# A layer step on one core: the running sums of the gates stored in DRAM by head and then by chunk

## The chip, the cores and the metric

The kernel runs on one core of one Trainium2 chip. The metric is the device time of one execution, in microseconds. Runs of one kernel differ by about 0.1% here: the three runs of the kernel before lie between 1456.16 and 1457.99 us.

## The reference, cut to what matters

One layer of a hybrid decoder is computed for a prompt of 1024 tokens and for 8 samples of one token each. All of it is float32. A combined projection `h @ w_in` (1024 to 10256 columns) feeds two branches. Branch B is a gated delta rule with 8 heads of 128 x 128, evaluated in chunks:

```python
proj = h @ w_in
hA, cA, bA, zA, qkv, zB, beta_raw, alpha_raw, gA, gB = jnp.split(proj, offs, axis=-1)
...
g = -jnp.exp(a_log) * jax.nn.softplus(alpha_raw + dt_bias)        # one number per token and head
...
gc = jnp.cumsum(g, axis=-1)                                       # running sum inside a chunk, per head
decay = jnp.exp(jnp.where(causal, gc[..., :, None] - gc[..., None, :], -jnp.inf))
a_mat = jnp.where(strict, jnp.einsum('bhncd,bhnsd->bhncs', kb, k) * decay, 0.0) + jnp.eye(C)
...
attn_qk = jnp.einsum('bhncd,bhnsd->bhncs', q, k) * decay
q_dec = q * jnp.exp(gc)[..., None]
```

So `gc` is needed twice for every head: as a row (the index s runs along a row of `decay`) and as a column. The change concerns the rows.

## The kernel before, in words

**Work and stages.** TensorE computes the projection as jobs of 128 columns. Each job has three groups of 344 tokens, and each float32 product is made of three passes of a rounded part and a remainder (`xh`/`xl` with `whi`/`wlo`), so a job is 3 x 8 x 3 matmuls into PSUM tiles called `pm_t`. For each head h there is a K, a Q and a V job, a job for a gate and one for z. Between about 90 and 815 us of the span these jobs run, and the delta rule of the heads runs between them: its matmuls write PSUM tiles called `pa_t`. From 815 us on come products of the second branch, the output projections and the tail, which do not use the part that is changed.

**Order.** Every engine works through its instructions in the order in which they were written. That order is settled when the program is made: `Sched` keeps a modelled clock of each engine, and generators ("strands", run by `slot()` after every k step of a job) are advanced when their modelled time has come. `Paced.__getattr__` adds to these clocks at every call. A `tensor_copy` on VectorE, for one, adds 100 ns and its elements per partition divided by 1.92; a DMA is modelled by its size alone, as 1100 ns, the bytes divided by 360, and 700 ns.

**The running sums.** `ba_gen` computes the gates once, near 85 us. A matmul with a triangular matrix gives `gc`, a tile of 128 partitions (position in the chunk) by 8 chunks by 8 heads (`gcf` is the same with 64 columns, chunk by chunk). TensorE transposes it to `gcr` (64 rows of 128), and SyncE (SP) writes that to `gsc` in DRAM, 64 rows of 512 bytes in the order chunk, head.

**The broadcasts.** `gc_rows(h)` is an access pattern that reads the 8 rows of head h and repeats them for all 128 partitions: 512 KB land in SBUF. It is loaded twice for every head, both times on SP's DMA queue. `decay_gen` (after the K job of the head) loads it into `DA`; ScalarE (ACT) adds the negated column to it in 8 instructions (`DA<-DA,ngc`), VectorE (DVE) masks it, and ACT takes the exponential, so that `DB` and `DA` become the two decay matrices. `delta_gen` loads it again into `gcB`; `qd_gen` lets ACT take the exponential and DVE multiply q by it. ACT and DVE also empty the PSUM tiles of the jobs, split the weights (`whi`, `wlo`), and do the small steps of the recurrence: `vn` is copied out of PSUM by ACT, and TensorE needs it for the next two matmuls (`pa_t<-vn,kd` and `pa_t<-vn,DA`). A head also has loads and stores that invert a triangular matrix through DRAM (`sA`, `At`, `sT`, `Ts`), and the samples' step has a broadcast of its own: `rsc[h]`, 8 rows of 128 that lie one after another, is written by SP and read back for all partitions into `rB`.

Nearly all instructions are recorded at line 128, the helper `Paced`, so the profile is read by tiles.

Of the kernel before, what the change touches and what calls it, by code (L numbers as in the profile page):

```python
# [8 lines left out]
F32 = mybir.dt.float32  # L9
# [7 lines left out]
P = 128  # L17
# [5 lines left out]
NH = 8  # L23
C = 128
NC = S // C
# [136 lines left out]
def hybrid_step(  # L162
# [9 lines left out]
    V, A, PE, GP, SY = (Paced(e, n, sched) for e, n in (  # L172
        (nc.vector, "V"), (nc.scalar, "A"), (nc.tensor, "PE"), (nc.gpsimd, "GP"), (nc.sync, "SY")))
# [9 lines left out]
    def ps_aux():  # L183
        return psum["pa"].tile([P, 512], F32, tag="pa", name="pa_t")

    def tt(out, a, b, op):
        V.tensor_tensor(out=out, in0=a, in1=b, op=op)

    def ts(out, a, s1, s2=None, op0=ALU.mult, op1=None):
        if s2 is None:  # L190
            V.tensor_scalar(out=out, in0=a, scalar1=s1, scalar2=None, op0=op0)
        else:
            V.tensor_scalar(out=out, in0=a, scalar1=s1, scalar2=s2, op0=op0, op1=op1)

    def stt(out, a, s, b, op0, op1):
        V.scalar_tensor_tensor(out=out, in0=a, scalar=s, in1=b, op0=op0, op1=op1)
# [6 lines left out]
    def act(out, in_, func, **kw):  # L203
        A.activation(out=out, in_=in_, func=func, **kw)
# [57 lines left out]
    gc = cpool.tile([P, NC, NH], F32, name="gc")  # L262
# [10 lines left out]
    gsc = dram.tile([NC * NH, C], F32, name="gsc")  # L273
# [11 lines left out]
    def transpose(out, in_):  # L285
        n = in_.shape[0]
        PE.transpose(out, in_, ident[:n, :n])
# [465 lines left out]
    def ba_gen():  # L753
        ap_ = bp
        ban = ap_.tile([P, 9, 16], F32, name="ban")
        GP.memset(ban, 0.0)
        pt = ps_aux()
        for i in range(9):
            n = P if i < 8 else NB
            transpose(pt[:n, 48 * i:48 * i + 48], ba[:, i * P:i * P + n])  # L760
        for n, i0, i1 in ((P, 0, 8), (NB, 8, 9)):
            pv = pt[:n, 48 * i0:48 * i1].rearrange("p (i n) -> p i n", n=48)
            V.tensor_copy(out=ban[:n, i0:i1, :], in_=pv[:, :, 0:16])
            tt(ban[:n, i0:i1, :], ban[:n, i0:i1, :], pv[:, :, 32:48], ALU.add)
        T4.give(ba_)
        al = ap_.tile([P, NH], F32, name="al")
        db = ap_.tile([P, NH], F32, name="db")
        SY.dma_start(out=al, in_=a_log.to_broadcast([P, NH]))
        SY.dma_start(out=db, in_=dt_bias.to_broadcast([P, NH]))
        act(beta, ban[:, :, 0:NH], AF.Sigmoid)  # L770
        yield
        xg = ap_.tile([P, 9, NH], F32, name="xg")
        u = ap_.tile([P, 9, NH], F32, name="u")
        sq = ap_.tile([P, 9, NH], F32, name="sq")
        pl = ap_.tile([P, 9, NH], F32, name="pl")
        tt(xg, ban[:, :, NH:16], db.unsqueeze(1).to_broadcast([P, 9, NH]), ALU.add)
        act(al, al, AF.Exp)
        stt(u, xg, -1.0, xg, ALU.mult, ALU.max)
        act(u, u, AF.Exp, scale=-1.0)
        ts(sq, u, 2.0, op0=ALU.add)  # L780
        V.reciprocal(out=sq, in_=sq)
        tt(u, u, sq, ALU.mult)
        tt(sq, u, u, ALU.mult)
        ts(pl, sq, 1.0 / 19)
        for n in (17, 15, 13, 11, 9, 7, 5, 3):
            stt(pl, pl, 1.0 / n, sq, ALU.add, ALU.mult)
        stt(pl, pl, 1.0, u, ALU.add, ALU.mult)
        ts(xg, xg, 0.0, op0=ALU.max)
        stt(xg, pl, 2.0, xg, ALU.mult, ALU.add)
        stt(xg, xg, -1.0, al.unsqueeze(1).to_broadcast([P, 9, NH]), ALU.mult, ALU.mult)  # L790
        yield

        pt = ps_aux()
        gv = xg[:, 0:8, :].rearrange("p c h -> p (c h)")
        PE.matmul(pt[:, 0:64], lhsT=triu, rhs=gv, start=True, stop=True)
        PE.matmul(pt[:, 64:128], lhsT=ones, rhs=gv, start=True, stop=True)
        gcf = gc.rearrange("p c h -> p (c h)")
        V.tensor_copy(out=gcf, in_=pt[:, 0:64])
        neg["gc"] = ngc = ap_.tile([P, NC, NH], F32, name="ngc")
        ts(ngc.rearrange("p c h -> p (c h)"), gcf, -1.0)  # L800
        tt(ekd.rearrange("p c h -> p (c h)"), pt[:, 64:128], gcf, ALU.subtract)
        act(egl.rearrange("p c h -> p (c h)"), pt[:, 64:128], AF.Exp)
        act(ekd, ekd, AF.Exp)
        act(egc, gc, AF.Exp)
        yield
        pt = ps_aux()
        transpose(pt[:64, 0:C], gcf)
        gcr = ap_.tile([64, C], F32, name="gcr")
        V.tensor_copy(out=gcr, in_=pt[:64, 0:C])
        SY.dma_start(out=gsc, in_=gcr)  # L810
        act(u[:NB, 0, :], xg[:NB, 8, :], AF.Exp)
        SY.dma_start(out=smp[0], in_=u[:NB, 0, :])
        SY.dma_start(out=smp[1], in_=beta[:NB, 8, :])
        SY.dma_start(out=gbs.rearrange("p a b h -> p (a b h)"),
                     in_=smp.rearrange("a b h -> (a b h)").unsqueeze(0).to_broadcast([P, 2 * NB * NH]))
        flags["ba"] = True
# [45 lines left out]

        jobs.append((w_in, c0, P, x_src, None, evac, after))

    gc_rows = lambda h: gsc.rearrange("(c h) i -> h c i", h=NH)[h].unsqueeze(0).to_broadcast([P, NC, C])
    waiting = set()

    def decay_gen(h, st):
# [968 lines left out]
    for g0, gn in GROUPS:  # L1837
# [5 lines left out]
        A.copy(out=ba[:, g0:g0 + gn], in_=ps[:48, :gn])  # L1843
    T4.give(wb_)
    start(ba_gen())
    run(jobs, 1, isp)
    products()
# [30 lines left out]
    for j in range(9):  # L1878
        i, n, xr, mh, ml, held = pre.pop(j)
# [33 lines left out]
        for half in range(2):  # L1913
            hs = slice(half * 512, (half + 1) * 512)
            stt(yt[:n, hs], yt[:n, hs], r, xr[:n, hs], ALU.mult, ALU.add)
            out = y_prompt[0, i * P:(i + 1) * P, hs] if i < 8 else y_sample[:, 0, hs]
# [38 lines left out]
```

## Time and profile before

| | |
|---|---|
| three runs | 1456.16, 1457.18 (median), 1457.99 us |
| the profiled execution | 1448.45 us, of which the span from the first to the last instruction is 1446.2 us |
| mean granted TensorE clock | 0.986 |
| TensorE busy (matmul) | 1387.4 us, 96% |
| VectorE, ScalarE busy | 988.2 us (68%), 680.7 us (47%) |
| DMA moved | 165.99 MB, 115 GB/s over the span |

A row of a timeline gives start and duration in us, the engine, the operation, the tile written and the tiles read, the shapes, and in brackets the idle time of the engine just before it with what ended it. SPq is SP's issue of a DMA. A row of the chain gives start, duration and what the chain of waits went through; for a DMA that is the time from its issue to its landing. A row of a table by stretch gives the stretch and its length, then the busy time of each engine (and its instructions), then the mean granted TensorE clock, the busy share of the 16 DMA engines and GB/s.

### The profile page before, as it was taken

To read this page: it belongs to the slowest core of one execution; us is meant where nothing else is said; L and a number is where in the kernel's file an instruction comes from. 1 tells how busy PE (TensorE), PEld (TensorE's weight loads), DVE (VectorE), ACT (ScalarE), POOL (GpSimd) and SP (SyncE) were. 2 spreads that over 40 slices of the span, in tenths; PEclk is the share of its full clock that TensorE was granted. 3 is DMA by queue.
4 is the path that set the end of the run, shared out by engine and by line. 5 is a ranking of instruction groups with operands and counts; after the bars stand their busy time and mean duration, and the time that the engine had idled before them with its cause. 6 is when DMAs were issued, how large, how long until landed. Compare 5 with 4: busy or idle time off the path is not lost.

```text
span 1446.2 us, 26424 instructions
## 1 busy us (share of the span) xinstructions
PE 1387.4 (96%) x10246; PEld 1333.5 (92%) x10246; DVE 988.2 (68%) x2516; ACT 680.7 (47%) x1536; POOL 43.0 (3%) x95
## 2 busy tenths in 40 slices
PE   6999989989989999999999999999999999999997
PEld 4899988989889888899999999999999999999786
DVE  6767856575676745868664699877777877964553
ACT  6765664565465644757443344322322445532211
POOL 0000000000000000000000000000000110000000
PEclk9999999999999998999999999999999999999999
DMA  9523342213333322434343445531123776653221
GB/s 322 152 49 105 91 97 81 67 57 81 84 100 85 104 60 63 116 77 97 92 117 106 148 132 191 172 108 53 47 63 89 210 245 220 212 158 103 90 88 58
DMA packets 200272, 165.99 MB, mean 115 GB/s; under 512 B 34734, under 2 KB 175775, under 8 KB 200139
## 3 DMA queue, kind: packets, MB, share of 16 engines
q1 hardware_dynamic: 195592, 155.77, 37.2%
q0 software_dynamic: 4352, 8.46, 2.0%
q8 instruction: 80, 1.31, 0.4%
q14 instruction: 46, 0.37, 0.1%
q10 hardware_dynamic: 202, 0.08, 0.0%
HBM read 127.59 MB, written 36.91 MB: 114 GB/s over the span
## 4 chain that ended last, share of the span: by engine, by line
PE 73%; DMA 11%; DVE 8%; ACT 4%; issue 2%; SPq 1%; DVEq 0%; POOL 0%; ACTq 0%
PE pm_t L128 49%; PE pa_t L128 22%; DMA gcB<-gsc 4%; DMA DA<-gsc 3%; PE pb L128 2%; DVE wlo L128 1%; SPq L128 1%; DVE Ts L128 1%; DVE vT L128 1%; DVE Ttmp L128 1%; DVE acc L128 1%; DMA Ts<-sT 1%; DMA xs<-in_x_prompt_dram 1%; ACT L128 1%; DMA sT<-Ts 1%
## 5 line engine op out<-in xcount | busy, mean ns | idle before, releaser
L128 PE MATMUL pm_t<-xh,whi 128*128 128x344 f32 (+1 forms) x1384 | 457.9, 331 | 0.0
L128 PE MATMUL pm_t<-xh,wlo 128*128 128x344 f32 (+1 forms) x1384 | 437.7, 316 | 2.1 <-DVE wlo L128 2.1
L128 PE MATMUL pm_t<-xl,whi 128*128 128x344 f32 (+1 forms) x1384 | 436.7, 316 | 0.0
L128 PEld LDWEIGHTS pm_t<-xh,wlo 128*128 128x128 f32 x1384 | 263.6, 190 | 2.7 <-DVE wlo L128 2.4
L128 PEld LDWEIGHTS pm_t<-xh,whi 128*128 128x128 f32 x1384 | 264.3, 191 | 1.8
L128 PEld LDWEIGHTS pm_t<-xl,whi 128*128 128x128 f32 x1384 | 264.1, 191 | 0.1
L128 ACT CAST whi<-wr 128x1024 fp32r<-128x1024 f32 x60 | 62.9, 1048 | 135.4 <-PE pa_t L128 65.9
L128 DVE TENSOR_TENSOR wlo<-wraw,whi 128x512 fp32r<-128x512 f32 x112 | 75.8, 686 | 37.0 <-ACT whi L128 36.3
L128 ACT CAST whi<-wraw 128x512 fp32r<-128x512 f32 x112 | 68.4, 625 | 45.8 <-PE pm_t L128 41.7
L128 PE MATMUL pa_t<-tlo,whi 128*128 128x258 f32 x304 | 85.9, 282 | 0.0
L128 PE MATMUL pa_t<-thi,wlo 128*128 128x258 f32 x304 | 85.8, 282 | 0.0
L128 PE MATMUL pa_t<-thi,whi 128*128 128x258 f32 x304 | 85.7, 282 | 0.0
L128 PE MATMUL pm_t<-tlo,whi 128*128 128x258 f32 x304 | 85.6, 282 | 0.0
L128 PE MATMUL pm_t<-thi,wlo 128*128 128x258 f32 x304 | 85.1, 283 | 0.5 <-DVE wlo L128 0.5
L128 PE MATMUL pm_t<-thi,whi 128*128 128x258 f32 x304 | 85.5, 282 | 0.0
L128 DVE TENSOR_TENSOR wlo<-wr,whi 128x1024 fp32r<-128x1024 f32 x60 | 73.2, 1219 | 11.5 <-ACT whi L128 11.3
L128 ACT ACT_TABLE_LOAD x43 | 55.2, 1283 | 39.6 <-DMA gcB<-gsc 24.3
L128 DVE SCALAR_TENSOR_TENSOR kq<-raw,vecs,kq 128x528 f32<-128x528 f32 x96 | 70.9, 762 | 2.3 <-ACT kq L128 2.1
L128 PE MATMUL pa_t<-xh,whi 128*128 128x258 f32 x256 | 72.4, 283 | 0.0
L128 PE MATMUL pa_t<-xl,whi 128*128 128x258 f32 x256 | 72.2, 282 | 0.0
L128 PE MATMUL pa_t<-xh,wlo 128*128 128x258 f32 x256 | 72.2, 282 | 0.0
L128 PE MATMUL pm_t<-yhi,wlo 128*128 128x344 f32 x192 | 61.4, 320 | 0.0
(395 smaller groups left out, 3076.4 us busy)
## 6 DMA issues: line engine op xcount, KB each, us to landing
wraw<-in_w_in_dram SPq DMA_DIRECT2D x48, 512.0 KB
wr<-in_w_in_dram SPq DMA_DIRECT2D x64, 256.0 KB
aw<-in_ada_w_dram SPq DMA_DIRECT2D x16, 512.0 KB
gBsc<-gate SPq DMA_DIRECT2D x8, 516.0 KB
gAsc<-gate SPq DMA_DIRECT2D x8, 516.0 KB
txs<-phi SPq DMA_DIRECT2D x8, 516.0 KB
txs<-plo SPq DMA_DIRECT2D x8, 516.0 KB
yAsc<-acc SPq DMA_DIRECT2D x8, 516.0 KB
```

The costliest lines, as they stand in the source:

```text
L128: r = f(*args, **kw)
```

## The change

`gc` is copied once more, on VectorE, into a tile `gch` whose 64 columns are ordered head by head instead of chunk by chunk. The transpose reads that copy, so the 64 rows written to `gsc` are in the order head, chunk. The 8 rows of one head then lie one after another, 4 KB in all, and `gc_rows(h)` reads them there. `gc`, `gcf` and what is computed from them stay.

```diff
         gcf = gc.rearrange("p c h -> p (c h)")
         V.tensor_copy(out=gcf, in_=pt[:, 0:64])
+        gch = ap_.tile([P, NH, NC], F32, name="gch")
+        V.tensor_copy(out=gch, in_=gc.rearrange("p c h -> p h c"))
...
         pt = ps_aux()
-        transpose(pt[:64, 0:C], gcf)
+        transpose(pt[:64, 0:C], gch.rearrange("p h c -> p (h c)"))
         gcr = ap_.tile([64, C], F32, name="gcr")
         V.tensor_copy(out=gcr, in_=pt[:64, 0:C])
         SY.dma_start(out=gsc, in_=gcr)
...
-    gc_rows = lambda h: gsc.rearrange("(c h) i -> h c i", h=NH)[h].unsqueeze(0).to_broadcast([P, NC, C])
+    gc_rows = lambda h: gsc.rearrange("(h c) i -> h c i", h=NH)[h].unsqueeze(0).to_broadcast([P, NC, C])
```

## The prediction

> **What bounds the kernel.** I read the page first: the busy shares, then the chain that ended last by line.
>
> ```profile
> PE 1387.4 (96%) x10246; PEld 1333.5 (92%) x10246; DVE 988.2 (68%) x2516; ACT 680.7 (47%) x1536; POOL 43.0 (3%) x95
> ...
> PE pm_t L128 49%; PE pa_t L128 22%; DMA gcB<-gsc 4%; DMA DA<-gsc 3%; PE pb L128 2%; DVE wlo L128 1%; SPq L128 1%; DVE Ts L128 1%; DVE vT L128 1%; DVE Ttmp L128 1%; DVE acc L128 1%; DMA Ts<-sT 1%; DMA xs<-in_x_prompt_dram 1%; ACT L128 1%; DMA sT<-Ts 1%
> ```
>
> TensorE (PE) bounds it. The two broadcasts of the running sums, `gcB<-gsc` and `DA<-gsc`, are the largest item of the chain that is not PE: 4% + 3%. That share is only a pointer, since a load can stand on the chain while PE works beside it. So the table by stretch comes next: the stage that holds the broadcasts, and the one after it.
>
> ```profile
> 90.00:815.00 725.00, 687.44 (x5215) 670.13 (x5214) 470.32 (x1585) 405.96 (x1128) 26.07 (x52) 0.98 0.34 88
> 815.00:1140.00 325.00, 325.00 (x2666) 324.94 (x2666) 266.80 (x415) 112.64 (x166) 0.00 (x0) 1.00 0.37 115
> ```
>
> After 815 us PE is never idle and its clock is 1.00; that stretch only starts earlier if this one ends earlier. From 90 to 815 us PE is idle for 725.00 - 687.44 = 37.6 us, and its mean clock is 0.98. These two are all that can be gained. Who holds PE? Third come the waits of ACT in this stage.
>
> ```profile
> ACT DA L128 <- DMA DA<-gsc: 26.8, 6, 8.2
> ACT L128 <- DMA gcB<-gsc: 24.3, 4, 7.7
> ACT gcB L128 <- DMA gcB<-gsc: 15.4, 4, 7.3
> ```
>
> ACT stands still for 26.8 + 24.3 + 15.4 = 66.5 us because one of these broadcasts has not landed (the middle row is a table load queued with the exponential). ACT works in order, so whatever stands behind waits too, `vn` above all. Fourth, the timeline: ACT's idle times that are followed by an idle time of PE, and then PE's.
>
> ```profile
> 192.71 1.28 ACT L128 ACT_TABLE_LOAD   x1 [5.96 <-DMA gcB<-gsc]
> 251.09 1.28 ACT L128 ACT_TABLE_LOAD   x1 [4.95 <-DMA gcB<-gsc]
> 296.07 0.40 ACT L128 ACTIVATE DA<-DA,ngc 128x128 f32<-128x128 f32 x1 [5.87 <-DMA DA<-gsc]
> 373.79 1.06 ACT L128 ACTIVATE gcB<-gcB 128x1024 f32<-128x1024 f32 x1 [5.42 <-DMA gcB<-gsc]
> 404.18 0.98 ACT L128 ACTIVATE DA<-DA,ngc 128x128 f32<-128x128 f32 x3 [4.66 <-DMA DA<-gsc]
> 542.24 1.28 ACT L128 ACT_TABLE_LOAD   x1 [7.68 <-DMA gcB<-gsc]
> 573.01 0.37 SPq L128 DMA_DIRECT2D DA<-gsc  x1
> 581.39 0.40 ACT L128 ACTIVATE DA<-DA,ngc 128x128 f32<-128x128 f32 x1 [5.49 <-DVE kq L128]
> ```
>
> ```profile
> 199.34 1.09 PE L128 MATMUL pa_t<-ident,kq 128*128 128x128 f32 x4 [5.93 <-DVE DA L128]
> 255.93 0.80 PE L128 MATMUL pa_t<-vn,kd 128*128 128x128 f32 x2 [5.20 <-ACT vn L128]
> 297.08 0.77 PE L128 MATMUL pa_t<-vT,DB 128*128 128x128 f32 x2 [4.06 <-ACT DB L128]
> 377.72 1.11 PE L128 MATMUL pa_t<-DB 64*64 64x64 f32 x16 [2.79 <-issue]
> 406.87 0.49 PE L128 MATMUL pa_t<-vn,kd 128*128 128x128 f32 x2 [2.38 <-ACT vn L128]
> 545.05 0.79 PE L128 MATMUL pa_t<-vn,kd 128*128 128x128 f32 x2 [5.80 <-ACT vn L128]
> 588.85 0.49 PE L128 MATMUL pa_t<-vn,kd 128*128 128x128 f32 x2 [3.00 <-ACT vn L128]
> ```
>
> The two lists pair off, one to one. At 255.93, say, PE waits for `vn`; ACT copies `vn` only behind the exponential of `gcB`, which began at 251.09 after 4.95 us of waiting. At 581.39 the profile names DVE, but the instruction reads `DA`, and it starts 8.4 us after that load's issue, about as long as such a load takes (below); I count it as the load. PE's seven waits are 29.2 of its 37.6 idle us.
>
> **The landing time.** The chain in order of time gives issue to landing for the old form, and once for the new: `rB<-rsc` reads one run of 4 KB for 128 partitions into a tile of the same shape on the same queue.
>
> ```profile
> 145.50 7.89 DMA DA<-gsc
> ...
> 182.52 10.13 DMA gcB<-gsc
> ...
> 241.31 9.69 DMA gcB<-gsc
> ...
> 286.45 9.53 DMA DA<-gsc
> ...
> 393.80 10.36 DMA DA<-gsc
> ...
> 533.10 9.07 DMA gcB<-gsc
> ...
> 581.21 3.73 DMA rB<-rsc
> ```
>
> The packets of one load of each kind, from the DMA view cut to 91.18 to 99.71 us (a `DA<-gsc`) and to 581.21 to 584.95 us (that `rB<-rsc`):
>
> ```profile
> DMA packets 1041, 0.53 MB, mean 62 GB/s; under 512 B 16, under 2 KB 1040, under 8 KB 1040
> ...
> DMA packets 144, 0.52 MB, mean 140 GB/s; under 512 B 16, under 2 KB 16, under 8 KB 144
> ```
>
> The same half megabyte goes as 1024 packets of 512 B in one form and as 128 of 4 KB in the other. The new pattern has `rB`'s strides, so I expect `rB`'s packets and 3.73 us. The bounds: no shortening at all at one end, and 10.36 - 3.73 = 6.6 us at the other. I take each load's own time less 3.73, because the nearest row is the same transfer in all but its source tensor.
>
> A rule stands against this. The Trainium skill, page "DMA: Bandwidth & Descriptors", section Specifications, gives 512 B as the smallest transfer for line rate; by that the old form has the full rate already, and the sum would be zero. The trace disagrees: 62 GB/s against 140 in the rows above.
>
> **Step by step, ACT and PE.** Each PE wait shrinks by the smallest of three: the shortening of the load, ACT's idle time behind it, and the wait itself.
> 193 us: shortening 6.4, ACT 5.96, PE 5.93, so 5.9. 251: 6.0, 4.95, 5.20, so 4.95. 292: 5.8, 5.87, 4.06, so 4.06. 374: the load isn't in my list; even at 7.89, the quickest of it, 4.2, against PE's 2.79, so 2.79. 404: 6.6, 4.66, 2.38, so 2.38. 539: 5.3, 7.68, 5.80, so 5.3. 585: the load took at most 581.39 - 573.01 = 8.4, so 4.6, ACT 5.49, PE 3.00, so 3.0. Sum 28.4 us.
> The broadcasts that hold ACT but no PE wait are worth nothing by themselves: PE has jobs to go on with, and that is their cover.
>
> **The clock.** After the longer waits PE comes back slower. The table by stretch, cut to begin where PE resumes:
>
> ```profile
> 199.34:210.00 10.66, 10.66 (x54) 10.30 (x55) 8.63 (x15) 9.97 (x30) 2.83 (x1) 0.75 0.60 163
> 255.93:260.00 4.07, 4.07 (x18) 4.07 (x19) 2.39 (x10) 3.50 (x12) 0.00 (x0) 0.58 0.01 4
> 297.08:310.00 12.92, 12.92 (x82) 12.90 (x82) 8.10 (x29) 9.52 (x22) 1.13 (x1) 0.88 0.16 42
> 377.72:390.00 12.28, 12.28 (x84) 11.70 (x85) 3.20 (x16) 5.63 (x15) 0.52 (x1) 0.72 0.17 45
> 545.05:560.00 14.95, 14.95 (x150) 13.77 (x151) 2.89 (x11) 6.74 (x29) 1.13 (x3) 0.74 0.19 53
> ```
>
> Length times the missing clock: 10.66 x 0.25 = 2.7, 4.07 x 0.42 = 1.7, 12.92 x 0.12 = 1.6, 12.28 x 0.28 = 3.4, 14.95 x 0.26 = 3.9; 13.3 us together, at full busy. With the waits gone I take all of it as gained; the bounds are 0 and 13.3.
> The Trainium skill, page "TensorE: Matmul & The Clock Gate", Part 1, says that the clock halves after an idle window of about 3.4 us and returns after a busy one. That fits four of the five rows; the 2.79 us wait at 374 is too short for it, and by the rule alone its 3.4 us would stay and the clock term would be 9.9. I keep the row's.
>
> **What is added.** One copy on DVE, once, 128x64 in and out of SBUF with a stride on one side.
>
> ```profile
> 85.77 0.21 DVE L128 COPY gc<-pa_t 128x64 f32<-128x64 f32 x1
> ...
> 86.58 0.19 DVE L128 TENSOR_SCALAR ngc<-gc 128x64 f32<-128x64 f32 x1
> ```
>
> Between 0.19 and, doubling the dearer row for the stride, 0.42 us; I take 0.2. Behind it on DVE stand `ngc`, `ekd` and the K conv of head 0, and, by way of the transpose, `gcr` and the write of `gsc`; the first load of `DA` may be issued 0.2 us later. The cover is that PE has no wait before 193 us, so it costs nothing, and at most 0.4. The transpose and the write of `gsc` are unchanged in shape, and SP issues the same DMAs. Small transfers queued on the same rings behind a broadcast (`rsc`, `sA`, `Ts<-sT`) get through sooner; I add nothing for them.
>
> **What is late next.** PE idles 37.6 - 29.2 = 8.4 us in this stage for other reasons, DVE and ACT among them. When PE no longer waits for the broadcasts, ACT and DVE have the same work in less time, and some of those waits will grow. An estimate: half as much again as the 8.4, about 5 us, comes back (bounds 0 and all).
>
> Sum: 28.4 + 13.3 - 5 = 36.7, say 37 us. Against the profiled execution's 1448.45 that is 1411.5. The median of the runs shown, 1457.18, is 8.7 above it; I carry that difference over: 1457.2 - 37 = 1420 us.
>
> **Rivals.** First, part of it comes back: PE meets the next wait within microseconds, and the clock drops that remain (PE needs only one longer wait in each place) keep their 13.3. For it: every PE wait above ends with ACT or DVE work that lies behind the load, not with the load. Then 28.4 less twice the 8.4 of other waits is about 12 (1445), and with half the clock term about 18 (1439); I count all gains of 10 to 30 us to this case. Against it: DVE is busy 470 and ACT 406 of the 725 us, so neither is short of time.
>
> Second, no change: the loads do not land sooner, as the 512 B rule above would have it, or the pattern isn't merged into 4 KB packets. Time 1457. Against it: `rB` has the same strides and went out in 128 packets.
>
> Third, slower. The added copy moves the modelled VectorE clock by 100 + 64 / 1.92 = 133 ns where the order of instructions is settled, and every strand after `ba_gen` can fall into another `slot()`. Place: everything after 86 us. Price: a badly placed step is a wait like the one at 545.05, 5.80 + 3.9 = 9.7 us. It needs four of these to eat 37 us and five to make the kernel slower, 1468; if the broadcasts gain only 12, two do. Against it: a shift of one slot moves a step by under half a microsecond.
>
> **Chances.** The forecast, a gain of 30 to 48 us (1409 to 1427): 0.62. Part of it, 10 to 30 (1427 to 1447): 0.22. More than 48, because the small transfers behind the broadcasts matter too: 0.04. A small gain of 3 to 10: 0.02. Within 2.9 us (0.2%, about what a measurement of this kernel can tell from no change): 0.04. Slower: 0.06. Faster is then 0.90. The range 1409 to 1442 leaves out the 0.04 below, the 0.12 of the last three and some of the second.
>
> **What would show it.** `DA<-gsc` and `gcB<-gsc` landing in about 4 us in packets of 4 KB; ACT's 66.5 us of waits for them under 15; PE's idle time in the stage under 15 us; the clock there at 0.99 to 1.00; the stretch after the stage unchanged. The prediction is wrong if the loads still take 9 us, if PE waits as long as before but for `vn` behind something else, or if the clock still halves in several places.

## The result and the profile after

| | before | after |
|---|---|---|
| median | 1456.67 us (1453.96 to 1457.99, 4 runs) | 1402.74 us (1401.22 to 1402.95, 4 runs) |
| profiled execution, its span | 1448.45 us, 1446.2 us | 1402.95 us, 1399.0 us |
| mean granted TensorE clock in it | 0.986 | 0.998 |

The ratio is 0.963 (95% interval 0.9613 to 0.9647): the kernel is 53.9 us faster. The forecast was a gain of 37 us, to 1420 us with a range of 1409 to 1442; the direction held, and the time lies 6 us below the range. One execution of before, beside e13 to e15, took 3449.89 us; it counts as slow and is left out everywhere.

The page of after, busy shares and chain by line, against the two lines shown first in the prediction:

```profile
PE 1372.5 (98%) x10246; PEld 1321.2 (94%) x10246; DVE 987.5 (71%) x2517; ACT 681.4 (49%) x1536; POOL 41.3 (3%) x95
...
PE pm_t L128 58%; PE pa_t L128 24%; PE pb L128 2%; DVE wlo L128 1%; DVE Ts L128 1%; DVE Ttmp L128 1%; DVE vT L128 1%; DVE acc L128 1%; DMA Ts<-sT 1%; SPq L128 1%; DMA xs<-in_x_prompt_dram 1%; DMA aw<-in_ada_w_dram 1%; DVE S L128 1%; DMA yAsc<-acc 0%; DMA sT<-Ts 0%
```

Both broadcasts have left this list of the chain; they held 7% of it. The table by stretch of after follows. Its first two rows hold the same matmuls as the prediction's two rows (5215 and 2666, so the stage now ends at 765 us), and the last is the tail.

```profile
90.00:765.00 675.00, 671.91 (x5215) 657.82 (x5214) 469.43 (x1585) 407.84 (x1128) 24.37 (x52) 1.00 0.33 94
765.00:1090.00 325.00, 325.00 (x2666) 324.94 (x2665) 266.83 (x415) 112.27 (x166) 0.00 (x0) 1.00 0.37 115
1090.00:1399.00 309.00, 298.55 (x1884) 274.07 (x1883) 191.55 (x364) 102.38 (x147) 11.61 (x16) 0.99 0.48 153
```

The stage is 725 - 675 = 50.0 us shorter. PE's idle time in it falls from 37.6 to 675.00 - 671.91 = 3.1 us, which is 34.5 us. PE's busy time falls from 687.44 to 671.91 for the same matmuls, 15.5 us: that is the clock, 0.98 to 1.00. The stretch after the stage is unchanged. The tail, which nothing in the change touches, took 306.2 us in the profiled execution of before:

```profile
1140.00:1446.20 306.20, 297.88 (x1881) 273.66 (x1880) 191.37 (x363) 102.66 (x146) 11.61 (x16) 0.99 0.48 155
```

So it is 2.8 us longer in after's, and 50.0 - 2.8 = 47.2 us is the difference of the spans.

What holds PE, and what holds ACT, from 85 to 780 us in after (engine, tile, what it waited for: us in total, times, longest):

```profile
PE pa_t L128 <- ACT vn L128: 2.2, 3, 1.4
PE pa_t L128 <- DVE S L128: 0.4, 1, 0.4
PE pa_t L128 <- DVE Ts L128: 0.2, 1, 0.2
PE pa_t L128 <- DVE DA L128: 0.2, 1, 0.2
...
ACT gcB L128 <- DMA gcB<-gsc: 4.7, 2, 3.5
ACT L128 <- DMA gcB<-gsc: 3.4, 2, 2.4
ACT DA L128 <- DMA DA<-gsc: 3.4, 3, 1.4
```

ACT waits 11.5 us for the broadcasts where it waited 66.5, and PE's seven long waits are gone. The one broadcast that still stands on after's chain in order of time, and the packets of the first load of `DA` (the DMA view cut to 92.11 to 95.76 us):

```profile
496.43 3.78 DMA gcB<-gsc
...
DMA packets 144, 0.52 MB, mean 144 GB/s; under 512 B 16, under 2 KB 16, under 8 KB 144
```

The same load, of head 5, took 9.07 us from issue to landing before (the row at 533.10 in the prediction). Over all 16 loads the median falls from 9.1 to 3.8 us, to what `rB<-rsc` took. What the loads and the waits do is as the prediction said, only larger. The experiments are about two questions: why the loads land sooner, and why the gain is 54 us and not 37. The expectations call the theories by letters; the text here tells them in words.

### The profile page after: what moved, and what is told of

Read it like the earlier page. It is cut to its first block, busy times and chain, and to the rows that moved or that the text cites. A ratio compares the mean times of both kernels' runs of the same rounds, so it can differ in the third digit from the quotient of the medians.

```text
span 1399.0 us, 26425 instructions
## 1 busy us (share of the span) xinstructions
PE 1372.5 (98%) x10246; PEld 1321.2 (94%) x10246; DVE 987.5 (71%) x2517; ACT 681.4 (49%) x1536; POOL 41.3 (3%) x95
## 3 DMA queue, kind: packets, MB, share of 16 engines
q1 hardware_dynamic: 181256, 155.77, 36.7%
## 4 chain that ended last, share of the span: by engine, by line
PE 84%; DVE 8%; DMA 5%; ACT 2%; issue 1%; SPq 1%; DVEq 0%; ACTq 0%
PE pm_t L128 58%; PE pa_t L128 24%; PE pb L128 2%; DVE wlo L128 1%; DVE Ts L128 1%; DVE Ttmp L128 1%; DVE vT L128 1%; DVE acc L128 1%; DMA Ts<-sT 1%; SPq L128 1%; DMA xs<-in_x_prompt_dram 1%; DMA aw<-in_ada_w_dram 1%; DVE S L128 1%; DMA yAsc<-acc 0%; DMA sT<-Ts 0%
## 5 line engine op out<-in xcount | busy, mean ns | idle before, releaser
L128 PEld LDWEIGHTS pm_t<-xh,whi 128*128 128x128 f32 x1384 | 261.0, 189 | 1.8
L128 PEld LDWEIGHTS pm_t<-xl,whi 128*128 128x128 f32 x1384 | 261.1, 189 | 0.1
L128 PEld LDWEIGHTS pm_t<-xh,wlo 128*128 128x128 f32 x1384 | 260.4, 188 | 0.2
L128 ACT ACT_TABLE_LOAD x43 | 55.2, 1283 | 18.2 <-DVE vT L128 5.3
```

Source lines behind the costliest of these rows:

```text
L128: r = f(*args, **kw)
```

## Experiments: the copy and the order

**Order undone (e1).** After, with the new copy hidden from the modelled clocks, so that the engines' instructions keep the order of before:

```diff
-        V.tensor_copy(out=gch, in_=gc.rearrange("p c h -> p h c"))
+        nc.vector.tensor_copy(out=gch, in_=gc.rearrange("p c h -> p h c"))
```

> The change with the extra copy hidden from the modelled clocks, so that all instructions stand in the order of the kernel before. Theory A (the loads land sooner, and PE's waits behind them and the half clock after those go): as the changed kernel, 1403 us within 3. Theory C (part of the gain is the new order): more than 3 us away from the changed kernel, towards 1457.

Measured 1401.61 us, ratio 0.9644 (0.9609 to 0.968). The new order is no part of the gain.

**The copy alone (e2).** The copy and the order of after, but the rows of `gsc` as before:

```diff
-        gch = ap_.tile([P, NH, NC], F32, name="gch")
-        V.tensor_copy(out=gch, in_=gc.rearrange("p c h -> p h c"))
+        gch = ap_.tile([P, NC // 1, NH, 1], F32, name="gch")
+        V.tensor_copy(out=gch, in_=gc.rearrange("p (a b) h -> p a h b", b=1))
```

(The transpose reads it in that order, and `gc_rows` stays as before.)

> The extra copy and the order of the changed kernel, but the rows lie as before (runs of 512 B). Theory A: as before, 1457 us within 4, with loads that land in about 9 us. Theory C: faster than 1450.

Measured 1452.08 us over 10 runs, ratio 0.999 (0.9968 to 1.0012). That is below the range expected, but so was the kernel before beside it (1454.67). The copy costs nothing that can be seen, and the whole gain comes from where the rows lie. The median landing is 9.0 us here. Its profiled execution is the longest of its ten (1461.11 us), which turns out to matter; its stage by stretch:

```profile
90.00:815.00 725.00, 686.32 (x5148) 670.27 (x5147) 464.99 (x1567) 404.01 (x1120) 25.37 (x52) 0.96 0.34 86
```

PE is idle for 725.00 - 686.32 = 38.7 us of it, much as in the profile of before (37.6), but the clock is 0.96 and not 0.98, and the stage isn't done (5148 matmuls, not 5215). Waits of the same length cost more clock in one execution than in another. One pair shows it: PE's wait for `vn` that ends at 596.59 us here, 2.79 us long, and the same wait in the profile of before, which ends at 588.85 and is 3.00 us long. The stretch around each, first e2, then before:

```profile
595.79:602.61 6.82, 6.02 (x24) 6.02 (x24) 3.18 (x12) 4.31 (x14) 0.21 (x1) 0.50 0.19 77
```

```profile
585.85:602.61 16.76, 13.76 (x94) 13.52 (x95) 14.75 (x38) 14.90 (x35) 0.21 (x1) 1.00 0.31 94
```

The shorter wait is followed by half clock, the longer one is not.

## Experiments: the two loads apart

Both layouts are written, through an extra transpose, copy and write to `gsc2` that the modelled clocks don't see; e3 lets only `gcB` read the new one, e4 only `DA`:

```diff
+        nc.tensor.transpose(pt[:64, C:2 * C], gch.rearrange("p h c -> p (h c)"), ident)
...
+        nc.vector.tensor_copy(out=gcr2, in_=pt[:64, C:2 * C])
+        nc.sync.dma_start(out=gsc2, in_=gcr2)
...
-        SY.dma_start(out=gcB.rearrange("p (c i) -> p c i", i=C), in_=gc_rows(h))
+        SY.dma_start(out=gcB.rearrange("p (c i) -> p c i", i=C), in_=gc_rows2(h))
```

> Both layouts are written to DRAM; only the 8 loads of gcB read the new one. Theory A, with the prediction's terms: 18.9 us of PE waits and 11.7 us of missing clock go, 30.6 of its 41.7; scaled to the measured 54 us that is 40, so 1417 us (1426 unscaled). Theory B (the gain is mostly that small transfers no longer queue behind a broadcast; each of the 16 loads counts alike): half, 1430 us.

> Both layouts are written; only the 8 loads of DA read the new one. Theory A: 9.4 us of PE waits and 1.6 us of missing clock go, 11.0 of 41.7; scaled, 14, so 1443 us (1446 unscaled). Theory B: half, 1430 us.

Measured: e3 1425.54 us, ratio 0.9803 (0.9765 to 0.984), 29 us; e4 1427.58 us, ratio 0.9822 (0.9787 to 0.9857), 27 us. The kernel before was at 1454.67 beside them. The halves are alike and their sum, 56, is about the whole. In the prediction the waits that belong to `gcB` (193, 251, 374, 539) with their clock come to 30.6 us and those of `DA` (292, 404, 585) to 11.0. So the sum for `gcB` came out near (29 for 30.6) and that for `DA` far too small (27 for 11.0). By the times alone, two equal halves also fit the rival of the small transfers, which expected 1430 us for both; the waits speak against it, as is shown here and under e8. PE's waits in e3 and then in e4, 85 to 815 us:

```profile
PE pa_t L128 <- ACT vn L128: 7.2, 4, 3.9
PE pa_t L128 <- ACT DB L128: 3.2, 1, 3.2
PE pa_t L128 <- POOL DB L128: 2.7, 1, 2.7
PE pa_t L128 <- DVE S L128: 2.6, 3, 1.4
PE pa_t L128 <- ACT Ts L128: 1.4, 1, 1.4
PE pa_t L128 <- DVE Ts L128: 0.4, 1, 0.4
PE pa_t L128 <- DVE DA L128: 0.2, 1, 0.2
```

```profile
PE pa_t L128 <- ACT vn L128: 10.1, 3, 4.8
PE pa_t L128 <- DVE DA L128: 3.3, 2, 3.2
PE pa_t L128 <- issue: 3.1, 1, 3.1
PE pa_t L128 <- DVE S L128: 1.0, 2, 0.7
PE pa_t L128 <- ACT junk L128: 0.4, 1, 0.4
PE pa_t L128 <- DVE Ts L128: 0.3, 1, 0.3
```

With the `gcB` loads quick, 17.7 us of waits remain; the prediction's list leaves 9.4 for `DA` and 8.4 of others, 17.8, and hits it. With the `DA` loads quick, 18.2 remain where the list leaves 19.7 for `gcB` and 8.4 of others. So quick `DA` loads remove 37.6 - 18.2 = 19.4 us of waits, not 9.4. Some of PE's waits in before over the same stretch show where the other 10 us were:

```profile
PE pa_t L128 <- ACT vn L128: 18.8, 7, 5.8
PE pa_t L128 <- DVE DA L128: 6.1, 2, 5.9
...
PE pa_t L128 <- DVE S L128: 2.4, 2, 1.5
PE pm_t L128 <- DVE wlo L128: 2.1, 1, 2.1
PE pa_t L128 <- ACT Ts L128: 0.8, 1, 0.8
```

`S`, `wlo` and `Ts` (5.3 us, and 0.2 more of a second `Ts` group) are 1.3 in e4; `vn` falls from 18.8 to 10.1, where its two waits in the list for `DA` (404 and 585) make 5.4; the longest wait for `DVE DA`, that at 193, which the list gives to `gcB`, falls from 5.9 to 3.2. That is 4.2 + 3.3 + 2.7, and explains the 10. So work that the profile names as late by itself, or as late because of the other load, was late because of these loads. The rest of e4's surplus of 16 us shows in no wait; medians can't be split into waits and clock.

And the waits that remain in e3 still cost clock. Four pieces of its stage by stretch, each beginning in or soon after a wait:

```profile
220.60:227.40 6.80, 6.56 (x65) 6.16 (x66) 6.56 (x22) 4.59 (x9) 0.00 (x0) 0.50 0.30 76
391.30:398.10 6.80, 5.43 (x21) 4.97 (x21) 6.49 (x22) 4.58 (x13) 0.00 (x0) 0.50 0.03 10
483.40:490.20 6.80, 6.80 (x53) 6.37 (x50) 4.62 (x20) 2.29 (x6) 0.40 (x1) 0.50 0.49 146
561.90:568.70 6.80, 5.10 (x20) 5.10 (x21) 4.07 (x14) 5.20 (x15) 0.21 (x1) 0.50 0.19 77
```

In each the clock is 0.50 for 6.8 us. Half of PE's 6.56 + 5.43 + 6.80 + 5.10 busy us is lost, 11.9 in all: nearly the prediction's whole clock term (13.3), in a kernel that has only half of the slow loads. So in this execution the `gcB` loads returned their waits, but little of the 11.7 us of clock that the prediction counts to them. The waits in question are short: 2.69 us, 2.62 and 1.37 close together, 1.45, 3.93. A wait of 3.22 us for `DB`, which ends at 287.07, is followed by no half clock at all:

```profile
283.85:298.00 14.15, 10.93 (x76) 10.80 (x77) 9.11 (x43) 10.42 (x24) 1.13 (x1) 1.00 0.18 48
```

## Experiments: why the loads land sooner

**The length of the runs (e5, e6) and the size of the packets (e7).** e5 and e6 order the rows so that a head has 4 runs of 1 KB, 8 KB apart, or 2 runs of 2 KB, 16 KB apart (`r` is 2 or 4):

```diff
-        gch = ap_.tile([P, NH, NC], F32, name="gch")
-        V.tensor_copy(out=gch, in_=gc.rearrange("p c h -> p h c"))
+        gch = ap_.tile([P, NC // r, NH, r], F32, name="gch")
+        V.tensor_copy(out=gch, in_=gc.rearrange("p (a b) h -> p a h b", b=r))
```

e7 cuts each row of after in two halves of 256 B that lie 512 B apart, so that nothing merges and a load is 2048 packets of 256 B:

```diff
-    gsc = dram.tile([NC * NH, C], F32, name="gsc")
+    gsc = dram.tile([2 * NC * NH, C], F32, name="gsc")
...
-        SY.dma_start(out=gsc, in_=gcr)
+        SY.dma_start(out=gsc.rearrange("(r s) j -> r s j", s=2)[:, :, 0:C // 2], in_=gcr.rearrange("r (s j) -> r s j", s=2))
```

> Runs of 1 KB (two chunks of a head side by side), the rest as the changed kernel. Landing by a line through 1024 packets (9.3 us) and 128 (3.8 us): 512 packets, about 6.2 us. Theory A (time goes by the landing): a shortening of 3.1 us of 5.5; the waits at 374, 404 and 585 go, 1 to 3 us stay at 193, 251 and 539, and these are too short to halve the clock: 1405 to 1415 us. Theory D (what counts is to pass some size of run): 1402 us within 3.

> Runs of 2 KB (four chunks). Landing by the same line: 256 packets, about 4.6 us. Theory A: 1402 to 1406 us. Theory D: 1402 us within 3.

> Runs of 256 B (each row in two halves with a gap between them in DRAM). Landing by the same line: 2048 packets, about 15.5 us, 6 us more than before. Theory A: at least seven waits longer by 6 us each, 42 us, and more waits where ACT stood still without PE, and more time at half clock: 1495 to 1540 us. If the bytes and not the packets set the landing: 1457 us within 5.

Measured: e5 1443.44 us, ratio 0.9936 (0.9916 to 0.9956), median landing 8.3 us; e6 1406.13 us, 0.9676 (0.9652 to 0.9701), 5.1 us; e7 1399.71 us, 0.9633 (0.961 to 0.9655), 4.4 us. Packets twice as large win little, packets half as large as before win everything; both expectations of e5 and both of e7 are missed. The first load of `DA` in e7 and in e5, DMA view from its issue to its landing:

```profile
DMA packets 2064, 0.52 MB, mean 145 GB/s; under 512 B 2064, under 2 KB 2064, under 8 KB 2064
```

```profile
DMA packets 529, 0.53 MB, mean 69 GB/s; under 512 B 16, under 2 KB 528, under 8 KB 528
```

2048 packets of 256 B go at 145 GB/s, 512 packets of 1 KB at 69. Neither the size nor the number of packets explains this.

**The distance of the runs (e9).** In e7 and in after, the pieces of a head spread over 4 KB; in before and e5 they all begin at the same place in it. e9 is the kernel before, in its order, without any copy; each row of `gsc` only gets a gap of 64 B behind it. The 8 runs of a head are still 512 B each, now 4608 B apart and not 4096:

```diff
-    gsc = dram.tile([NC * NH, C], F32, name="gsc")
+    gsc = dram.tile([NC * NH, C + 16], F32, name="gsc")
...
-        SY.dma_start(out=gsc, in_=gcr)
+        SY.dma_start(out=gsc[:, 0:C], in_=gcr)
...
-    gc_rows = lambda h: gsc.rearrange("(c h) i -> h c i", h=NH)[h].unsqueeze(0).to_broadcast([P, NC, C])
+    gc_rows = lambda h: gsc.rearrange("(c h) i -> h c i", h=NH)[h][:, 0:C].unsqueeze(0).to_broadcast([P, NC, C])
```

e10 goes the other way: the kernel before with 16 pieces of 256 B for each head, all exactly 4096 B apart (`gsc` is written in 16 small DMAs).

```diff
+    gsc = dram.tile([2 * NC, 16, C // 2], F32, name="gsc")
+    gc_rows = lambda h: gsc[:, h, :].unsqueeze(0).to_broadcast([P, 2 * NC, C // 2])
```

> The kernel before, same order of all instructions and the same runs of 512 B in the order chunk, head; only each row in DRAM is followed by a gap of 64 B, so that the 8 runs of a head are 4608 B apart and not 4096. Theory E (the landing goes by how many different places modulo 4 KB the runs touch: one before, eight here): landing about 4 us in 1024 packets, and 1400 us within 5. Theory A (the landing goes by the number of packets or the size of a run) and theory F (runs must lie close together): as before, 1453 us within 5.

> Runs of 256 B as in the kernel with 256 B, but 4096 B apart, so all 16 runs of a head at one place modulo 4 KB. Theory E: landing 9 us or more, 1450 to 1540 us. If runs of 256 B are quick wherever they lie: 1400 us within 5.

Measured: e9 1399.8 us, ratio 0.9626 (0.9597 to 0.9656): the whole gain of the change. e10 1489.44 us, ratio 1.0231 (1.0199 to 1.0264). The first load of `DA` in e9 in the DMA view, and its load of `gcB` of head 5 on the chain:

```profile
DMA packets 1040, 0.52 MB, mean 146 GB/s; under 512 B 16, under 2 KB 1040, under 8 KB 1040
...
496.33 4.17 DMA gcB<-gsc
```

The same load on the chain of e10:

```profile
553.28 12.18 DMA gcB<-gsc
```

1024 packets of 512 B, the very packets of before, now go at 146 GB/s where they went at 62 (the prediction's row). With 256-B pieces the load takes 12.18 us when they lie 4096 B apart, and about 4.4 (e7) when they lie 512 B apart. It is the distance.

**Other distances (e13, e14, e15).** After, with its runs of 512 B kept apart by 1024, 2048 or 4160 B (`w` is 256, 512 or 1040):

```diff
-    gsc = dram.tile([NC * NH, C], F32, name="gsc")
+    gsc = dram.tile([NC * NH, w], F32, name="gsc")
...
+    gc_rows = lambda h: gsc[h * NC:(h + 1) * NC, 0:C].unsqueeze(0).to_broadcast([P, NC, C])
```

> The order of the changed kernel, runs of 512 B that lie 1024 B apart (a gap behind each row), so the 8 runs of a head touch four places modulo 4 KB. Theory E, by the runs of 2 KB that also touch four: landing about 4.7 us and about 1406 us. Theory G (only runs at exactly the same place modulo 4 KB hinder each other, all else is quick): 3.8 us and 1402.

> Runs of 512 B that lie 2048 B apart: two places modulo 4 KB. Theory E, by the runs of 1 KB that also touch two: landing about 8.5 us and about 1443 us. Theory G (each place is hit by four runs): half of the excess, about 6.5 us and 1415 to 1425 us.

> Runs of 512 B that lie 4160 B apart: each begins 64 B further on modulo 4 KB, so the eight together cover 960 B of the 4 KB. Theory E (places of 512 B: two): landing about 8.5 us, about 1443 us. Theory G (no two runs begin at the same place): 4 us and 1400 us.

Measured 1400.53 us (0.9629, 0.9611 to 0.9646), 1409.27 (0.9695, 0.9668 to 0.9722) and 1434.91 (0.9865, 0.9847 to 0.9884). All layouts side by side, by where the pieces of one head begin within 4 KB. The landing is the median of the 16 loads, issue to last completion in the trace:

| kernel | pieces of one head | where they begin, modulo 4 KB | landing, us | median, us |
|---|---|---|---|---|
| e10 | 16 x 256 B, 4096 B apart | one place | 12.6 | 1489.4 |
| before | 8 x 512 B, 4096 B apart | one place | 9.1 | 1456.7 |
| e5 | 4 x 1 KB, 8 KB apart | one place, 1 KB long | 8.3 | 1443.4 |
| e15 | 8 x 512 B, 4160 B apart | eight, 64 B apart | 7.9 | 1434.9 |
| e14 | 8 x 512 B, 2048 B apart | two, 2 KB apart | 5.5 | 1409.3 |
| e6 | 2 x 2 KB, 16 KB apart | one place, 2 KB long | 5.1 | 1406.1 |
| e7 | 16 x 256 B, 512 B apart | eight, 512 B apart | 4.4 | 1399.7 |
| e9 | 8 x 512 B, 4608 B apart | eight, 512 B apart | 4.2 | 1399.8 |
| e13 | 8 x 512 B, 1024 B apart | four, 1 KB apart | 4.0 | 1400.5 |
| after | 1 x 4 KB | all of it | 3.8 | 1402.7 |

On the whole, the more the pieces spread over 4 KB, the sooner the load lands, and the time of the kernel follows the landing down to about 4.4 us; the four quickest kernels differ by no more than their executions do. Yet no simple count fits, and e14 was forecast by neither theory. If only pieces with the very same beginning got in each other's way, e15 would be quick; it takes 7.9 us. If only the number of 512-B places touched mattered, e14 (two places) would equal e5 (1 KB, so two places as well); it takes 5.5 against 8.3. Which bits of the address decide stays open.

**Small transfers behind the loads (e8).** A quicker broadcast might also help by letting small transfers queued behind it through. After, with 16 extra 512-KB transfers in runs of 512 B (DRAM to DRAM, results unused), meant to stand behind each load:

```diff
+        nc.sync.dma_start(out=dum[2 * h], in_=old_rows(h))
...
+        nc.sync.dma_start(out=dum[2 * h + 1], in_=old_rows(h))
```

> The changed kernel, and behind each of the 16 loads a second transfer of 512 KB in runs of 512 B on the same queue, to DRAM, that nobody reads: the loads land early, but small transfers queue behind such a transfer as before. Theory A: within 5 us of the changed kernel, 1400 to 1408. Theory B (the small transfers behind): 1420 us or more.

Measured 1474.31 us, ratio 1.0149 (1.0125 to 1.0173), but the test failed. The extra transfers depend on `gsc` alone, and the build put almost all of them on SP's queue between 92 and 192 us, ahead of that queue's own work. One wait of PE in the waits from 85 to 300 us shows it:

```profile
PE pm_t L128 <- ACT last_q L128: 51.1, 1, 51.1
```

Of the 72 us that this kernel takes longer than after, 51.1 are this one wait. So the run says nothing on small transfers. The kept traces do. ACT's and DVE's waits for `Ts<-sT`, a small load on the same queue, from 85 to 815 us, first in before, then in e9:

```profile
DVE Ts L128 <- DMA Ts<-sT: 11.8, 6, 5.1
ACT T L128 <- DMA Ts<-sT: 10.0, 4, 5.2
```

```profile
ACT T L128 <- DMA Ts<-sT: 4.7, 3, 2.0
DVE Ts L128 <- DMA Ts<-sT: 2.8, 4, 1.2
```

They fall from 21.8 to 7.5 us. Likewise, of the 12 stores `sA<-DB` that were issued while a broadcast was under way, 8 took 7.5 to 8.7 us from issue to last completion in before, and none over 3.6 in e9. So small transfers do land sooner. But this is not where PE's time went, as far as e3 and e4 tell: in e3 the two rows fall to 9.6 us and PE's waits shrink by 37.6 - 17.7 = 19.9 us, just 1.0 more than the prediction's list for `gcB`; in e4 they only fall to 16.0 and PE gains 10 us more than the list. What the small transfers alone are worth stays open.

**One slow load put back (e11, e12).** All loads new, but `gcB` of head 5, or `DA` of head 5, reads the old layout:

```diff
-        SY.dma_start(out=gcB.rearrange("p (c i) -> p c i", i=C), in_=gc_rows2(h))
+        SY.dma_start(out=gcB.rearrange("p (c i) -> p c i", i=C), in_=(gc_rows if h == 5 else gc_rows2)(h))
```

> Both layouts are written; all loads read the new one, but the gcB of head 5 (issued at 533 us in the profile of before) reads the old one. The prediction's terms for it: 5.3 us of PE wait and 3.9 us of missing clock, so about 1411 us against 1401.6. If a wait costs only itself: 1407.

> The same with the DA of head 5 (issued at 573 us in the profile of before) on the old layout. The prediction's terms for it: 3.0 us of PE wait and no missing clock, so about 1404.6 us. If waits of this size also cost the clock in most executions: 1407 to 1409.

Measured: e11 1408.29 us, ratio 0.9684 (0.9653 to 0.9714); e12 1402.26 us, 0.9635 (0.9608 to 0.9661). Against e1, which has all loads new, that is 6.7 and 0.7 us (e1 ran on another chip; e11 and e12 also write the second layout, as e3 does). 0.7 us is less than what executions of one kernel differ by. The expectation of e12 names the wrong load: `DA` of head 5 is the one issued at 473.78 us in before, not at 573.01, which is head 6. For the load at 473.78 the prediction has no wait of PE, so its price there is nothing. The median can't be told from that, but the profile of e12 shows a price. PE's one wait between the issue of the slow load and that of the next `gcB<-gsc`, and the stretch between these two issues, in e12 and then in after:

```profile
467.32 1.50 PE L128 MATMUL pa_t<-Ts 32*32 32x32 f32 x48 [1.36 <-ACT Ts L128]
```

```profile
439.02:499.03 60.01, 58.65 (x458) 57.27 (x458) 40.58 (x131) 35.50 (x93) 2.35 (x6) 0.97 0.31 76
```

```profile
439.40:496.43 57.03, 57.03 (x458) 55.89 (x458) 40.46 (x131) 35.82 (x93) 2.33 (x6) 1.00 0.29 80
```

For the same matmuls e12 takes 3.0 us more: a wait of 1.36 us, and 1.6 us of clock. ACT waits 4.92 us for the load, so its work on `vT` and the work on `vT` that DVE does next are late, ACT's copy of `Ts` behind them comes 3.4 us later (466.91 against 463.52 us), and PE waits for that copy. In before, PE's waits of 2.14 us for `wlo` and 0.84 for `Ts`, which end at 496.86 and 502.39, stand at the same place behind the same load.

For e11 the prediction's price is 5.3 + 3.9 = 9.2 us. Its load on the chain, PE where it resumes, and the stretch of the halved clock:

```profile
496.36 9.30 DMA gcB<-gsc
...
508.54 0.80 PE L128 MATMUL pa_t<-vn,kd 128*128 128x128 f32 x2 [6.03 <-ACT vn L128]
...
504.76:521.83 17.07, 13.29 (x113) 12.42 (x114) 2.39 (x6) 7.98 (x29) 0.61 (x2) 0.50 0.35 97
```

One load that lands 5.5 us late (9.30 against 3.78) makes PE wait 6.03 us for `vn`, as the prediction has it for this place. From inside this wait on the clock stands at 0.50 for 17 us. PE works through all of the 13.29 us from 508.54 on, so some 6.6 us more are lost: 12.6 us in this execution. It took 1413.22 us, the other three of the kernel 1407.13 to 1409.20, so the same wait seems to have cost them some 6 us less; they have no profile that would show it.

## Why the prediction was wrong, and where it was right

**Right.** What bounds: PE, held by ACT, held by the broadcasts, and only between 90 and 815 us. The landing time taken from `rB` (3.73 forecast, 3.8 measured). The signs named for it: ACT's waits under 15 us (11.5), PE's idle time in the stage under 15 (3.1), clock 1.00 there, the stretch behind it unchanged. The copy at nothing (e2). In its example of a pair of waits, the row at 251.09 is the table load, and the exponential begins at 252.38; the order of waits is as it says. The third rival, slower by order, is refuted by e1 and e2. The second, no change by the rule on 512 B, did not come, and neither did the first, part of the gain coming back. The gain of 54 us fell into the class above 48 us, to which the prediction gave 0.04, with small transfers as the reason; they do land sooner, but the runs do not show that they are the reason.

**Wrong: why the loads land sooner.** The step read the size of the packets off two rows, 1024 of 512 B at 62 GB/s and 128 of 4 KB at 140, and took it for the cause. Two things differed between these loads: the packets, and the distance of the runs. e9 keeps the packets and changes the distance, and has the whole gain; e7 has packets of half the size, spread over 4 KB, and loses nothing. The landing time came out right by luck as far as the cause goes: `rB`, whose row was taken, has both the large packets and the runs side by side, and so has the new layout. The sentence "the trace disagrees" was wrong as well: at 4608 B the 512-B packets go at 146 GB/s.

The Trainium skill, page "DMA: Bandwidth & Descriptors", section Specifications (512 B for line rate), is thus borne out by e9 for packets of 512 B: 146 GB/s, against 144 for those of 4 KB in after. e7's 256-B packets, at 145 GB/s, show next to none below that size here (4.4 us against e9's 4.2). Nearer to the cause is a row of the same page's section "Latency and other measured facts": copies of 128 rows whose distance in DRAM is a large power of two slow down (207 GB/s at 512 KiB, 103 at 4 MiB), and a padding by 4 KiB restores the rate while one by 192 B does not. The runs here agree in kind, at a distance of 4 KiB and with all 128 partitions reading the same runs: 512 B of padding restores the rate (e9, 4.2 us), 64 B does not (e15, 7.9 us).

**Wrong in size: what is late next (-5 us).** The prediction let 5 us come back, from other waits growing. They shrank: of the 8.4 us, for `S`, `Ts`, `wlo` and the rest of `vn`, at most 3.1 are left, so this term should have been a gain of 5 us or more. Idle time fell by 34.5 us, not by 28.4 - 5 = 23.4. This is the largest miss, 11.1 us. As to waits, e3 and e4 place it: the `gcB` loads were worth what the list says, the `DA` loads 10 us of waits more (the two gains overlap: 19.9 and 19.4 us make 39.3, and both changes together removed 34.5). The step that failed is the sentence that broadcasts which hold ACT but no wait of PE are worth nothing by themselves, together with the term that lets 5 us come back. e12 shows the path for one such load: ACT is late for its next work, here the copy of `Ts`, and PE waits for that further on, 3.0 us with the clock in the profiled execution. That all 10 us of e4 came about in this way is argued from the waits that vanished (`S`, `wlo`, `Ts`, part of `vn`), not shown one by one.

**Near in size: the clock.** 13.3 us were forecast and 15.5 measured between the two profiled executions. Of the 2.2 between them, 1.6 is a stretch of half clock that the prediction's table leaves out: 3.41 us from 498.26 on, behind the 2.14 us wait for `wlo`, with PE busy for 3.29 of it. With 34.5 + 15.5 - 2.8 (the tail) these explain the 47.2 us between the spans.

**Wrong: the step from the profile to the median.** The prediction carried the 8.7 us by which the median lay above the profiled execution over to after. The executions of before beside the experiments (34) lie between 1448.59 and 1460.09 us, a spread of 0.8% and not of the 0.1% that three runs suggested, at clocks of 0.978 to 0.986, median 0.982; the profiled one, at 0.986, was among the quickest. After's profiled execution lies within 0.3 us of its median. By an estimate from these clocks, 0.004 of 1450, about 6 us of the excess was clock that the waits cost in most executions; it went with the waits (after's executions have 0.996 to 0.998). e2's profile, at 1461.11 us with the same idle time and a stage clock of 0.96, shows such an execution. That the whole of the excess was clock isn't shown.

These sizes add up: 11.1 (idle time) + 2.2 (clock) - 2.8 (tail) - 1.7 (by which the profiled times differ less than their spans, 45.5 and 47.2) + 8.4 (by which the medians differ more than the profiled times, 53.9 and 45.5) is 17.2 us, the distance from the forecast of 36.7 to the gain of 53.9.

## What to carry to other kernels

When many partitions read the same few rows from DRAM, look at the distance of the rows before the size of the packets: eight 512-B rows exactly 4 KB apart cost 5 us per 512-KB load here, and a gap of 64 B behind each 512-B row (e9), with no copy and no new order, bought the same 54 us as the new layout. (After, e1, e7, e9 and e13 lie between 1399.7 and 1402.7 us on different chips; none is shown to be the best.) When two rows of a trace differ in speed, list everything in which they differ, and change one thing at a time. A load that holds an engine without holding the bottleneck at once can still make a later step late: look at what that engine does next. And where a stall also costs clock, don't carry a profile's distance from the median over to the new kernel: it may be part of what the change removes.

## What the runs showed of the hardware

- A broadcast of 512 KB from 4 KB of DRAM takes 3.8 to 12.6 us by where its pieces lie within 4 KB; packets of 256 B to 4 KB make no difference of more than 0.6 us once the pieces are spread (e7, e9, after). The rule by which addresses collide is not settled.
- The granted clock halves in or behind waits of PE of 1.4 us (e12, e3) to 6 us, but not each time: not around the 3.22 us wait in e3 nor the 3.00 us wait in before. Between 90 us and the end of the jobs, the stretches at 0.50 in the traces of before, e2, e3, e4, e11 and e12 last 3.41, 6.83, 10.24 or 17.07 us, which is one, two, three or five times 3.41. So what a wait costs beyond its own length comes in steps of at most 1.7 us, and the length of the wait alone does not tell how many. In the same part of after there is none.
- In e11 the clock stays at 0.50 for 17.07 us, though PE works without a pause from 508.54 us to the end of this stretch, 13.3 us. The Trainium skill, page "TensorE: Matmul & The Clock Gate", Part 1, lets the clock return after some 3.4 us of sustained work; this one took nearly four times that.
